# Sending every fourth row group of a column roll through SBUF

## The chip, the cores and the metric

The kernel runs on one core of a Trainium2 chip. A core has compute engines (TensorE, VectorE, ScalarE or ACT, GpSimd or POOL, SyncE or SP), an on-chip memory of 128 partitions (SBUF), and 16 DMA engines that move data between SBUF and the off-chip memory (HBM) or from HBM to HBM. SP, ACT and GpSimd each issue transfers on a queue ("ring") of their own, and each of the 16 DMA engines serves packets from all the rings. The metric is the device time in microseconds; the figure for a kernel is the median of several runs.

## The reference

```python
def setup_inputs():
    return {
        "x": np.random.randn(8192, 8192).astype(np.float32),
        "shift": 100,
    }

def reference(x, shift):
    return np.roll(x, shift, axis=1)
```

Every row of 8192 floats is rotated to the right by 100: the last 100 columns of `x` become the first 100 of the output. Nothing is calculated. 268.4 MB have to be read and 268.4 MB written.

## The kernel before

The columns of the output are cut at column `a` = 256. With a shift `s` of 100, `a` is the shift rounded up to a multiple of 128, plus 128; `g = a - s` = 156.

**The body, output columns 256 to 8191.** These come from `x` columns 156 to 8091, and are copied from HBM to HBM directly (line 43). The rows are cut into 128 blocks `c` of 64 rows, and each block into four groups `j`. A group has 16 rows (`e`), four rows apart, of 7936 floats: 16 pieces of 31,744 bytes, 496 KB in all, one piece for each DMA engine. There are 512 groups. Even `j` go to SP's ring and odd `j` to ACT's. In the last four blocks every group is cut into two halves by columns (at `mid`), which makes 16 groups into 32 transfers. So each ring gets 248 whole transfers and 16 halves. The compiled program makes each of these transfers wait until the transfer four places before it on its own ring has landed.

**The edge, output columns 0 to 255.** These hold the wrapped columns (0 to 99) and the first 156 columns of `x`. They go through SBUF on GpSimd's queue, in 16 tiles of 512 rows. For each tile there are three loads: most of it in one strip that runs across row ends, into `t` (line 72), the wrapped part of each fourth row into `h` (line 73), and the first 156 columns of each fourth row into `h` (line 76). VectorE then copies the parts of `t` into place in `h` (lines 74 and 77). The pools `reads` (for `t`) and `heads` (for `h`) have one buffer for each of the 16 tiles, so no load waits for a buffer. After all the loads are issued, 16 stores write the tiles to the output (line 80).

The two parts write different columns and nothing of one waits for the other. Only the DMA engines and HBM are shared.

Of the kernel before, what the change touches and what calls it, by code (L numbers as in the profile page):

```python
# [1 line left out]

# [4 lines left out]


@with_exitstack
def kernel(  # L10
    ctx: ExitStack,
    tc: tile.TileContext,
    x: bass.AP,
    shift: int,
    out: bass.AP,
):
    nc = tc.nc
    n_rows, n_cols = x.shape
    s = shift % n_cols
    a = -(-s // 128) * 128  # L20
    if 0 < a <= 384 and a + 128 <= n_cols:
        a += 128
    g = a - s
    P = nc.NUM_PARTITIONS
    engines = [nc.sync, nc.scalar]
    n_chunks = 16
    rows = n_rows // n_chunks

    xm = x.rearrange("(c e j) w -> c j e w", e=16, j=4)
    om = out.rearrange("(c e j) w -> c j e w", e=16, j=4)
    if a < n_cols:
        blocks = n_rows // 64
        mid = (a + n_cols) // 256 * 128
        for c in range(blocks):
            parts = ((a, mid), (mid, n_cols)) if c >= blocks - 4 and a < mid else ((a, n_cols),)  # L40
            for j in range(4):
                for lo, hi in parts:
                    engines[j % 2].dma_start(out=om[c, j, :, lo:hi], in_=xm[c, j, :, lo - s:hi - s])
    if a == 0:
        return


    if a > 512:
        for i in range(n_chunks):
            r = slice(i * rows, (i + 1) * rows)  # L50
            nc.gpsimd.dma_start(out=out[r, :s], in_=x[r, n_cols - s:])
            if g > 0:
                nc.gpsimd.dma_start(out=out[r, s:a], in_=x[r, :g])
        return

    Q = 4  # L60
    n_st = n_rows // (P * Q)
    reads = ctx.enter_context(tc.tile_pool(name="reads", bufs=n_st))
    heads = ctx.enter_context(tc.tile_pool(name="heads", bufs=n_st))
    xt = x.rearrange("(k p q) c -> k p q c", q=Q, p=P)
    ot = out.rearrange("(k p q) c -> k p q c", q=Q, p=P)
    tiles = []
    for k in range(n_st):
        t = reads.tile([P, Q - 1, a], x.dtype)
        h = heads.tile([P, Q, a], x.dtype)
        lead = bass.AP(tensor=x.tensor, offset=(k * P * Q + 1) * n_cols - s,  # L70
                       ap=[[Q * n_cols, P], [n_cols, Q - 1], [1, a]])
        nc.gpsimd.dma_start(out=t[:], in_=lead, single_packet=True)  # L72
        nc.gpsimd.dma_start(out=h[:, Q - 1, :s], in_=xt[k, :, Q - 1, n_cols - s:], single_packet=True)  # L73
        nc.vector.tensor_copy(h[:, :Q - 1, :s], t[:, :, :s])  # L74
        if g > 0:
            nc.gpsimd.dma_start(out=h[:, 0, s:], in_=xt[k, :, 0, :g], single_packet=True)  # L76
            nc.vector.tensor_copy(h[:, 1:, s:], t[:, :, s:])  # L77
        tiles.append(h)
    for k, h in enumerate(tiles):
        nc.gpsimd.dma_start(out=ot[k, :, :, :a], in_=h[:], single_packet=True)  # L80


# [1 line left out]
_INS = ['x', 'shift']  # L84
_OUTS = [((8192, 8192), 'float32')]

_NUMBERS = {'shift': 100}


# [26 lines left out]
```

## Time and profile before

| | |
|---|---|
| median of 3 runs | 818.49 us (817.95 to 818.54) |
| span of the profiled execution, first to last instruction | 813.9 us |
| GpSimd busy | 41.1 us, 68 instructions |
| VectorE busy | 12.0 us, 32 instructions |
| DMA packets | 22277, 276.90 MB, mean 340 GB/s |
| row copy, issue to landing | 12.5 us (median of 248 on each of SP and ACT), 496 KB each |
| half row copy, issue to landing | 5.9 us (16 on each ring) |
| edge store on GpSimd's queue, issue to landing | 102.9 us (median of 16), 512 KB each |
| first edge store issued | 255.5 us |
| last edge store issued | 403.4 us |
| sequencer time to issue one row copy | 510 ns on SP, 517 ns on ACT |

The span counts the instructions that the profiler recorded; what lies before the first and after the last of them is not in it. A DMA engine is counted as busy from the start of a packet to its end, whatever holds the packet up in between. The row "DMA" of the page gives this busy share for 40 equal slices of the span, and the row "GB/s" what was moved in each. A copy from HBM to HBM is counted once in GB/s, although it is both a read and a write of HBM; the page's last DMA row gives HBM's own reads and writes. The DMA view can be asked for any stretch of the span, and then gives each queue's packets, its MB and its share of the 16 engines' time in that stretch. Half of the packets of SP's and ACT's rings are of 4 bytes: each transfer ends on each engine with a write to a semaphore.

### The profile page before, as it was taken

The page shows a single profiled execution, that of the slowest core. Times are in us where ns is not written, and L with a number is a line of the kernel's source. Part 1 is how long each engine was busy: PE and PEld are TensorE (multiplying, and loading weights), DVE is VectorE, ACT ScalarE, POOL GpSimd, SP SyncE. Part 2 cuts the span into 40 slices and gives each one's busy share as a digit, 9 for nine tenths or more (in the row PEclk, how much of TensorE's full clock was granted, in tenths as well). Part 3 has the DMA queues.
Part 4 walks back from the last instruction along what each step waited for, and adds up shares of the span by engine and source line. Part 5 has one row for each costly group of instructions (what it writes and reads, how often), then busy time and mean ns, then how long its engine had stood idle before and what let it go on. Part 6 is the DMA issues. An engine that isn't in the chain of part 4 may idle for free. (4 is left out here: it accounts for less than half of the span.)

```text
span 813.9 us, 689 instructions
## 1 busy us (share of the span) xinstructions
DVE 12.0 (1%) x32; POOL 41.1 (5%) x68
## 2 busy tenths in 40 slices
DVE  0000000000000000000000000000000000000000
POOL 2000011111000100000000000000000000000000
DMA  9999999999999999999999999999999999999998
GB/s 314 346 340 344 353 346 350 344 351 344 346 355 346 345 362 354 353 357 354 355 355 349 342 335 331 335 332 325 335 328 332 334 337 334 332 337 332 334 314 293
DMA packets 22277, 276.90 MB, mean 340 GB/s; under 512 B 9472, under 2 KB 9728, under 8 KB 13824
## 3 DMA queue, kind: packets, MB, share of 16 engines
q1 hardware_dynamic: 8448, 130.04, 45.9%
q10 hardware_dynamic: 8448, 130.04, 44.3%
q0 software_dynamic: 5376, 16.78, 8.9%
q14 instruction: 5, 0.04, 0.0%
HBM read 268.44 MB, written 268.44 MB: 660 GB/s over the span
## 5 line engine op out<-in xcount | busy, mean ns | idle before, releaser
L80 POOL DMA_DIRECT2D out_dram<-h x16 | 11.4, 713 | 139.5 <-DMA out_dram<-h 92.5
L76 POOL DMA_DIRECT2D h<-in_x_dram x16 | 8.6, 540 | 158.4 <-DMA t<-in_x_dram 158.4
L72 POOL DMA_DIRECT2D t<-in_x_dram x16 | 12.2, 760 | 32.1 <-DMA h<-in_x_dram 31.3
L73 POOL DMA_DIRECT2D h<-in_x_dram x16 | 8.9, 558 | 32.7 <-DMA h<-in_x_dram 32.7
L74 DVE COPY h<-t 128x300 f32<-128x300 f32 x16 | 5.9, 367 | 268.4 <-DMA t<-in_x_dram 268.4
L77 DVE COPY h<-t 128x468 f32<-128x468 f32 x16 | 7.5, 468 | 0.0
L97 POOL MEMSET const-float32-0.0<- 128x1 f32 x1 | 0.1, 98 | 0.2 <-issue 0.2
L97 POOL MEMSET const-bfloat16-1.0<- 128x1 bf16 x1 | 0.1, 101 | 0.0
L97 POOL MEMSET const-float32-1.0<- 128x1 f32 x1 | 0.1, 98 | 0.0
L97 POOL MEMSET const-uint8-127<- 128x1 uint8 x1 | 0.1, 98 | 0.0
## 6 DMA issues: line engine op xcount, KB each, us to landing
out_dram<-in_x_dram ACTq DMA_DIRECT2D x248, 496.0 KB, 12.5
out_dram<-in_x_dram SPq DMA_DIRECT2D x248, 496.0 KB, 12.5
out_dram<-h POOLq DMA_DIRECT2D x16, 512.0 KB, 102.9
t<-in_x_dram POOLq DMA_DIRECT2D x16, 384.0 KB, 48.9
out_dram<-in_x_dram SPq DMA_DIRECT2D x16, 248.0 KB, 5.9
out_dram<-in_x_dram ACTq DMA_DIRECT2D x16, 248.0 KB, 5.9
h<-in_x_dram POOLq DMA_DIRECT2D x16, 78.0 KB, 41.9
h<-in_x_dram POOLq DMA_DIRECT2D x16, 50.0 KB, 47.2
```

The costliest lines, as they stand in the source:

```text
L72: nc.gpsimd.dma_start(out=t[:], in_=lead, single_packet=True)
L73: nc.gpsimd.dma_start(out=h[:, Q - 1, :s], in_=xt[k, :, Q - 1, n_cols - s:], single_packet=True)
L74: nc.vector.tensor_copy(h[:, :Q - 1, :s], t[:, :, :s])
L76: nc.gpsimd.dma_start(out=h[:, 0, s:], in_=xt[k, :, 0, :g], single_packet=True)
L77: nc.vector.tensor_copy(h[:, 1:, s:], t[:, :, s:])
L80: nc.gpsimd.dma_start(out=ot[k, :, :, :a], in_=h[:], single_packet=True)
L97: nc = _bacc.Bacc("TRN2", target_bir_lowering=False, num_devices=1)
```

## The change

The row groups are numbered in their old order and worked through in two rounds and a remainder. A round has 32 turns of three copies and one load, and then 32 turns of three copies and one store. The loads bring one group each (16 rows of 31,744 bytes) into SBUF; the stores write these groups to the output. So in each round 224 groups are done, 192 as copies and 32 through SBUF. Both rounds do 448 groups, 64 of them (1024 rows) through SBUF; the remaining 64 groups are copied as before, with the last 16 in halves.

Transfers alternate between SP and ACT, so that the fourth of each turn, the load or the store, is always ACT's. As compiled, SP has 280 whole copies and 16 halves; ACT has 152 whole copies, 16 halves, 64 loads and 64 stores, each load or store next to a copy.

A slab is an SBUF tile of 128 partitions by 7936 floats and holds eight groups. Group `n` takes the partitions `n % 8`, `n % 8 + 8`, and so on to 16 partitions. There are four slabs, 32 groups, and the second round uses them again.

To make room in SBUF the pools of the edge get 9 buffers instead of 16. So the edge's first stores are now issued among the loads: from the ninth tile on a store follows (line 121 of the changed kernel), and the last eight stores come at the end (line 123). In the compiled order of GpSimd's queue the first of these stores stands behind the loads of the ninth tile, and from the tenth tile on the load of `h` at line 114 waits for the store of the tile nine before it to land.

```diff
-        for c in range(blocks):
+        groups = [(c, j) for c in range(blocks) for j in range(4)]
+        held = 32 if 0 < a <= 512 and n_cols <= 8192 and blocks >= 16 else 0
+        pool = ctx.enter_context(tc.tile_pool(name="rows", bufs=4)) if held else None
+        width = n_cols - a
+        turn = 0
+
+        def issue(to, of):
+            nonlocal turn
+            engines[turn % 2].dma_start(out=to, in_=of)
+            turn += 1
+
+        def copy(c, j):
             parts = ((a, mid), (mid, n_cols)) if c >= blocks - 4 and a < mid else ((a, n_cols),)
-            for j in range(4):
-                for lo, hi in parts:
-                    engines[j % 2].dma_start(out=om[c, j, :, lo:hi], in_=xm[c, j, :, lo - s:hi - s])
+            for lo, hi in parts:
+                engines[turn % 2].dma_start(out=om[c, j, :, lo:hi], in_=xm[c, j, :, lo - s:hi - s])
+            issue_done()
...
+        def load(n, c, j):
+            if n % 8 == 0:
+                slabs.append(pool.tile([nc.NUM_PARTITIONS, width], x.dtype, name="slab"))
+            w = slabs[-1][n % 8::8, :]
+            issue(w, xm[c, j, :, a - s:n_cols - s])
+            return w
+
+        slabs = []
+        at = 0
+        for _ in range(2 if held else 0):
+            kept = []
+            for n in range(held):
+                for _ in range(3):
+                    copy(*groups[at])
+                    at += 1
+                kept.append((groups[at], load(n, *groups[at])))
+                at += 1
+            for (c, j), w in kept:
+                for _ in range(3):
+                    copy(*groups[at])
+                    at += 1
+                issue(om[c, j, :, a:], w)
+        for g_ in groups[at:]:
+            copy(*g_)
...
-    reads = ctx.enter_context(tc.tile_pool(name="reads", bufs=n_st))
-    heads = ctx.enter_context(tc.tile_pool(name="heads", bufs=n_st))
+    depth = min(n_st, 9)
+    reads = ctx.enter_context(tc.tile_pool(name="reads", bufs=depth))
+    heads = ctx.enter_context(tc.tile_pool(name="heads", bufs=depth))
...
-    for k, h in enumerate(tiles):
-        nc.gpsimd.dma_start(out=ot[k, :, :, :a], in_=h[:], single_packet=True)
+        if k >= depth - 1:
+            nc.gpsimd.dma_start(out=ot[k - depth + 1, :, :, :a], in_=tiles[k - depth + 1][:], single_packet=True)
+    for k in range(n_st - depth + 1, n_st):
+        nc.gpsimd.dma_start(out=ot[k, :, :, :a], in_=tiles[k][:], single_packet=True)
```

More of the change, by code (lines that the diff above doesn't have):

```diff
@@ L38, with issue_done @@
         mid = (a + n_cols) // 256 * 128
-        for c in range(blocks):
-            parts = ((a, mid), (mid, n_cols)) if c >= blocks - 4 and a < mid else ((a, n_cols),)
-            for j in range(4):
-                for lo, hi in parts:
-                    engines[j % 2].dma_start(out=om[c, j, :, lo:hi], in_=xm[c, j, :, lo - s:hi - s])
+        groups = [(c, j) for c in range(blocks) for j in range(4)]
[8 more added lines that the diff above has]
+        def copy(c, j):
+            parts = ((a, mid), (mid, n_cols)) if c >= blocks - 4 and a < mid else ((a, n_cols),)
+            for lo, hi in parts:
+                engines[turn % 2].dma_start(out=om[c, j, :, lo:hi], in_=xm[c, j, :, lo - s:hi - s])
+            issue_done()
+        def issue_done():
+            nonlocal turn
+            turn += 1
+        def load(n, c, j):
[21 more added lines that the diff above has]
+            copy(*g_)
     if a == 0:
```

## The prediction

> **What bounds the kernel now.** I read the page's engine part first. VectorE is busy 12.0 us and GpSimd 41.1 us of a span of 813.9 us, so no compute engine matters. The chain of waits is of little use here: it follows GpSimd's queue and stops at 403.41 us, half the span before the end. So I went to the DMA rows:
>
> ```profile
> DMA  9999999999999999999999999999999999999998
> GB/s 314 346 340 344 353 346 350 344 351 344 346 355 346 345 362 354 353 357 354 355 355 349 342 335 331 335 332 325 335 328 332 334 337 334 332 337 332 334 314 293
> q1 hardware_dynamic: 8448, 130.04, 45.9%
> q10 hardware_dynamic: 8448, 130.04, 44.3%
> q0 software_dynamic: 5376, 16.78, 8.9%
> HBM read 268.44 MB, written 268.44 MB: 660 GB/s over the span
> ```
>
> The 16 DMA engines always have a packet in hand: 45.9 + 44.3 + 8.9 = 99.1% of their time. q1 and q10 are the rings of SP and ACT (which is which does not matter here), q0 is GpSimd's. The bytes per second are not constant: about 350 GB/s while q0 runs, about 332 after. "Busy" engines may still be held up by something outside them, so I compared stretches with and without q0's traffic. The DMA view for 50 to 250 us, for 300 to 400 us, and for 550 to 800 us:
>
> ```profile
> q1 hardware_dynamic: 1979, 31.40, 41.5%
> q10 hardware_dynamic: 1978, 31.37, 39.3%
> q0 software_dynamic: 2470, 6.75, 19.0%
> ```
>
> ```profile
> q1 hardware_dynamic: 978, 15.52, 46.0%
> q10 hardware_dynamic: 980, 15.59, 42.2%
> q0 software_dynamic: 1181, 4.30, 12.4%
> ```
>
> ```profile
> q1 hardware_dynamic: 2761, 41.38, 49.5%
> q10 hardware_dynamic: 2755, 41.59, 49.2%
> ```
>
> A byte of q1 or q10 is read from HBM and written to HBM; a byte of q0 touches HBM once, with SBUF on its other side. HBM traffic is thus 2 x (q1 + q10) + q0: (2 x 62.77 + 6.75) MB / 200 us = 661 GB/s, (2 x 31.11 + 4.30) / 100 = 665, and 2 x 82.97 / 250 = 664. Three stretches, three mixes, one HBM rate, while the bytes through the engines go 348, 354, 332 GB/s. The packet records say the same: the shortest packet of 31,744 bytes takes 1.173 us, the mean is 1.507 us from 550 to 780 us (20% under 1.18 us) and 1.348 us from 50 to 400 us (39%). The engines are stretched by what lies behind them. HBM traffic sets the time, and the engines have room: 16 x 31,744 B / 1.173 us = 433 GB/s at their shortest packet.
>
> **The change, part by part.** 64 of the 512 row groups (64 x 507,904 B = 32.5 MB) stop being one copy each and become a load into SBUF and, 64 ACT transfers later, a store. HBM traffic stays at 536.9 MB. The engines carry 32.5 MB more: 576 full packets for each engine where there were 512.
>
> *The legs.* Price of a copied MB, from the last stretch: 250 / 82.97 = 3.013 us. Price of an SBUF MB, as what the other stretches leave: (200 - 62.77 x 3.013) / 6.75 = 1.61 us and (100 - 31.11 x 3.013) / 4.30 = 1.46 us; both together 1.55. Half of a copy would be 1.51. A staged MB costs two legs: 2 x 1.55 - 3.01 = 0.09 us more, times 32.5 = **+3 us**. The ends by the two rows are +7 and -3 us.
>
> *The engines' room.* If HBM stays at 664 GB/s, three copies and one leg (seven HBM units, four engine units) need 664 x 4/7 = 379 GB/s of engine work, and 394 where q0 adds its 34 GB/s; the trace shows at most 354 without loss. In time: each engine has 512 packets in the two rounds and 64 in the remainder. With q0's 72 us (8.9% of 813.9) as they are and the remainder at 1.507 us, the 512 must average about (810 - 72 - 96) / 512 = 1.25 us, close to the shortest, 1.173. From below the loss is 0, as the step from 332 to 354 GB/s lost nothing. From above: if packets get no quicker than the 1.348 us already seen, 512 x 1.348 + 96 + 72 = 858 us, against 99.1% of 813.9 = 807 now, +52. I take **+7 us**, nearer to the rows that lost nothing but not on them, since the room left is about a third of what it was in the mixed stretch (0.08 against 0.175 us over the shortest). This choice is a judgement.
>
> *Issues.* SP issues 296 transfers instead of 264, ACT the same 296. At 0.51 us each that is 151 us of 814, hidden under the 12.5 us to landing of the four transfers in flight on each ring; uncovered, the 32 more would cost 16 us on each. In the compiled order every ring transfer waits for the one four places before it on its ring, before and after. The added waits are weak: a store stands 64 ACT transfers behind its load, some 170 us at 810 us / 296 = 2.7 us each; the second round's first load stands 50 behind the last store out of its slab, some 130 us. Were one late, ACT's later copies would queue behind it while SP went on. Cost 0.
>
> *GpSimd's queue.* With 9 buffers, the edge stores of L80 start among the loads, and from the tenth tile on each load of h waits until the store of the tile nine before has landed; behind it in that queue stand the next loads and stores, and VectorE's copies wait for those loads. As compiled these waits come in four pairs. At most each costs one landing (102.9 us): nine tiles take about 9/16 of 255 us = 143 us, plus 4 x 103, plus the last eight stores at 102.9 us = 658 us. The cover is the row copies, which run to the end; past 814 us every microsecond would count. Cost 0.
>
> Sum: 813.9 + 3 + 7 = 824 us of span. The runs' median is 818.49, 4.6 us over this span, for start and last landing outside it. Forecast: **828 us**.
>
> **Rivals.**
> (a) *SBUF side too narrow.* A load goes to 16 partitions, eight apart, one row from each engine. If two engines share a way into SBUF, a leg takes up to 2 x 1.173 = 2.35 us. 128 legs at 2.35 = 301, 448 copies at 1.18 = 529, q0 between 40 (its 4,096-byte packets at their median 0.16 us, scaled to 16.78 MB) and 72: 870 to 902 us, plus 4.6. Half of the legs meeting gives 128 x 1.76 + 529 + 56 = 810 with every copy at its shortest, and with these at 1.25 us 841, so 845. For: no transfer of this trace goes to so few partitions. Against: the other ring lets engines drift apart. The point from which it decides: legs above about 1.5 us. I work with 850 to 885.
> [...]
> (b) *Faster: a leg costs less than half a copy.* The legs are packets of 31,744 B, q0's are of 4 KB or less, and a staged row is read and written at different times. For: the 300 to 400 us row (1.46). Against: the other. As far below half as the 1.61 row lies above gives -7 us and no loss of room: **811**; twice that is 804.
> (c) *The engines are the bound after all*, a leg costing a packet like a copy: 576 x 1.434 (90.2% of 813.9 / 512) + 72 = 898, so 903. For: 99.1% busy. Against: the three HBM sums.
> That the change is not what it says is excluded by the compiled order: 64 loads and 64 stores alternate with copies on ACT.
>
> **How the numbers follow.** Forecast 0.52 (its own range 816 to 842), (a) 0.14, (b) 0.29, (c) 0.05. A measurement of this kernel tells about 0.2%, 1.6 us, from no change. Forecast: 0.41 slower, 0.08 within, 0.03 faster; (b): 0.02 within, 0.27 faster; (a) and (c) slower. Together slower 0.60, same 0.10, faster 0.30. Range 805 to 868: down to nearly twice (b), up into (a); (c), the rest of (a) and a bit of (b) stay out.
>
> **What would show it.** Right: HBM traffic near 655 GB/s and engine bytes of 370 to 390 GB/s in the rounds (to about 690 us), 332 after; packet mean near 1.27 us in the rounds; q0 done before 660 us. (a): packets of ACT's ring much longer than SP's, with a group near 2.3 us. (b): HBM traffic above 670 GB/s in the rounds. (c): engine bytes stay at 350 or below. Wrong altogether: gaps in the DMA row, or a queue other than the two rings landing last.

## The result, and the profile after

The changed kernel takes 825.75 us (median of 5 runs, 823.73 to 830.82) where the kernel before took 818.49 us on the same chip (817.95 to 818.62). The ratio is 1.0104, with a 95% interval of 1.0073 to 1.0136: about 7 us slower by the medians. The profiled execution is the slowest of the five, 830.82 us with a span of 829.0 us. The runs spread over 7.1 us, where those of the kernel before spread over 0.67 us here and over 2.1 to 5.5 us on the chips of the experiments. In the experiments, a ratio leaves out runs that took over 1.5% longer than the fastest of their kernel, and a time in us is the median of all runs.

The DMA rows of the page:

```profile
DMA  9999999999999999999999999999999999999998
GB/s 316 353 363 354 352 361 391 386 401 383 384 392 402 382 389 392 391 396 381 404 398 392 396 379 377 377 378 382 385 380 377 381 378 378 378 354 325 326 314 300
q10 hardware_dynamic: 9472, 146.30, 47.1%
q1 hardware_dynamic: 9472, 146.30, 46.5%
q0 software_dynamic: 5376, 16.78, 6.1%
HBM read 268.44 MB, written 268.44 MB: 648 GB/s over the span
```

The engines are as busy as before and HBM moves the same bytes; q1 and q10 carry 32.5 MB more. The GB/s row has three levels: 352 to 363 in the slices from 21 to 124 us, 381 to 404 up to 476 us, 377 to 385 up to 725 us, the end of the rounds. A slice is 20.7 us. The view of the tile `slab` shows which stage is where (columns: issue time in ns, then start of the first and the last):

```profile
L47 ACTq DMA_DIRECT2D slab<-in_x_dram x64: 515/522/866, 1.4 to 551.3; - x64
L47 ACTq DMA_DIRECT2D out_dram<-slab x64: 527/527/537, 193.5 to 722.7; - x64
DMA to landing us min/median/max: 8.7/11.2/14.0
```

The first round's loads run from 1.4 to about 190 us. So the low level covers the first half of these loads, and ends with no stage of the kernel.

To see what HBM did, the bytes need a weight. A copy touches HBM twice, a load or a store once: 2 x 227.54 MB of copies, 65.01 MB of loads and stores and 16.78 MB of the edge make 536.87 MB, and the page has 2 x 268.44 = 536.88. In the rounds one of four ring transfers is a load or a store, so four parts through the rings are seven parts of HBM. HBM traffic in the rounds is therefore 7/4 x (q1 + q10) + q0, and before it was 2 x (q1 + q10) + q0. The DMA view from 20 to 115 us, of the changed kernel and then of the kernel before:

```profile
q10 hardware_dynamic: 967, 15.21, 46.4%
q1 hardware_dynamic: 974, 15.43, 41.6%
q0 software_dynamic: 1112, 3.03, 12.2%
```

```profile
q1 hardware_dynamic: 939, 14.92, 40.8%
q10 hardware_dynamic: 936, 14.83, 39.5%
q0 software_dynamic: 1143, 3.11, 19.5%
```

(7/4 x 30.64 + 3.03) / 95 us = **596 GB/s** after, (2 x 29.75 + 3.11) / 95 = **659 GB/s** before. In these 95 us the changed kernel moved 56.65 MB of HBM traffic where the other moved 62.61: it fell behind by 5.96 MB, which at 659 GB/s is 9.0 us. The changed kernel from 350 to 500 us, and then from 520 to 740 us:

```profile
q10 hardware_dynamic: 1676, 26.70, 45.9%
q1 hardware_dynamic: 1678, 26.67, 45.5%
q0 software_dynamic: 1513, 5.29, 9.4%
```

```profile
q1 hardware_dynamic: 2628, 41.75, 50.7%
q10 hardware_dynamic: 2624, 41.56, 49.3%
```

That is (7/4 x 53.37 + 5.29) / 150 = 658 and 7/4 x 83.31 / 220 = 663 GB/s, against 661 to 665 in the stretches of the kernel before that the prediction used. So of the 15.1 us by which the two profiled spans differ, 9.0 arose from 20 to 115 us. The first 20 us add 1.7 us (10.9 MB of HBM traffic against 12.1 MB), and some 5 us came at a slightly lower rate from 115 to 500 us (252.6 MB against 255.8 MB). Once GpSimd's queue is empty, at 499 us, the rounds run at HBM's old rate. The medians differ by only half of 15.1 us: this profile is of the slowest of the five runs, and that of the kernel before is of a run faster than all five timed ones (813.9 us of span and some 1.8 us around it). So the figures of this section show where the loss lies, and overstate how large it usually is.

Why the first loads? The packet records give durations. At the start the 16 engines are in step (the 16 packets of the first load start within 0.7 us of one another), so that the whole packets of ACT's ring, sorted by start and cut into sixteens, are its transfers one by one; every second is a load. By the fifth load the starts lie 2.5 us apart, so the later columns are less sure. The first five loads took, in us as a mean of 16 packets:

```
                                    load 1  load 2  load 3  load 4  load 5
changed kernel, step of 8 partitions  1.96    1.92    1.91    2.04    1.74
step of 8, 28 groups held             1.87    1.85    1.78    1.68    1.60
step of 7, 28 groups held             1.74    1.75    1.72    1.35    1.39
step of 1                             3.66    3.54    3.28    3.41    2.85
changed kernel without the edge       1.99    1.82    1.61    1.43    1.34
kernel before, copies in these places 1.52    1.24    1.28    1.35    1.28
```

The copies between these loads on the same ring (q10) took 1.18 us in the changed kernel, and 1.23 us the first of them, close to the shortest packet, 1.173 us. In step, a load is the slow transfer. The last row shows that the first place is slow even for a plain copy. The rows between are of the experiments.

The long packets last as long as the low level of the GB/s row. From 20 to 115 us, 18% of ACT's whole packets took over 1.9 us and their mean was 1.46 us, against 1.29 us on SP's ring; from 130 to 190 us, with the same round of loads still running, 2% did.

### The profile page after: what moved, and what is told of

The parts are those of the page before. It is cut to its first block, busy times and chain, and to the rows that moved or that the text cites. A ratio compares the mean times of both kernels' runs of the same rounds, so it can differ in the third digit from the quotient of the medians.

```text
span 829.0 us, 762 instructions
## 1 busy us (share of the span) xinstructions
DVE 12.0 (1%) x32; POOL 41.5 (5%) x68
## 3 DMA queue, kind: packets, MB, share of 16 engines
q0 software_dynamic: 5376, 16.78, 6.1%
HBM read 268.44 MB, written 268.44 MB: 648 GB/s over the span
## 6 DMA issues: line engine op xcount, KB each, us to landing
out_dram<-slab ACTq DMA_DIRECT2D x64, 496.0 KB, 10.9
```

## The experiments

Three groups of runs were made on chips where the kernel before took 817.06, 828.81 and 828.51 us, and one run on a chip where it took 829.31, so ratios are compared, not times.

### The partitions that a load goes to

Two kernels differ only in the step between partitions. A slab takes seven groups so that both fit.

```diff
-        held = 32 if 0 < a <= 512 and n_cols <= 8192 and blocks >= 16 else 0
+        held = 28 if 0 < a <= 512 and n_cols <= 8192 and blocks >= 16 else 0
-            if n % 8 == 0:
+            if n % 7 == 0:
-            w = slabs[-1][n % 8::8, :]
+            w = slabs[-1][n % 7:n % 7 + 106:7, :]     # step of 7
+            w = slabs[-1][n % 7::8, :]                # or: step of 8, the control
```

> The changed kernel with 28 groups held in a round instead of 32, seven to a slab, and a load's 16 rows seven partitions apart instead of eight. In the changed kernel's profile the first loads, with the 16 engines in step, take 1.91 to 2.04 us a packet where the copies beside them take 1.18 to 1.4. Theory A (the 16 partitions share too few ways into SBUF): a step of seven shares fewer, so the first loads fall towards 1.2 to 1.4 us, HBM traffic from 20 to 115 us rises from 596 to about 650 GB/s and the loss of 7 us shrinks to 0 to 3: 818 to 822 us. Theory B (the engines have too little room left, wherever the rows go): no difference from the same kernel with a step of eight, about 825 us, HBM traffic from 20 to 115 us near 600 GB/s. [...]

> The control for the step of seven: 28 groups held in a round, seven to a slab, rows eight partitions apart. Both theories: like the changed kernel, 824 to 826 us, first loads near 1.9 to 2.0 us, HBM traffic near 600 GB/s from 20 to 115 us.

Step of seven: 819.83 us, ratio 1.0034 (1.0021 to 1.0047). Step of eight: 822.31 us, ratio 1.0074 (1.0052 to 1.0096); that is below the 824 to 826 us expected of the control. The DMA view from 20 to 115 us, step of seven and then step of eight:

```profile
q1 hardware_dynamic: 1066, 16.92, 44.0%
q10 hardware_dynamic: 1057, 16.64, 43.1%
q0 software_dynamic: 1176, 3.19, 12.9%
```

```profile
q10 hardware_dynamic: 1028, 16.32, 46.4%
q1 hardware_dynamic: 1027, 16.29, 43.4%
q0 software_dynamic: 1116, 2.99, 10.7%
```

HBM traffic is (7/4 x 33.56 + 3.19) / 95 = 652 GB/s with a step of seven and 632 with eight, where 600 was expected of the control. Each is of the slowest run of its kernel, and two kernels with a step of eight gave 596 and 632, so the times weigh more than these rates. The intervals of the ratios do not overlap, and nothing but the partitions differs: about half of the control's loss hangs on where the rows land in SBUF. The first loads did not fall as far as theory A expected: three at 1.72 to 1.75 us, not 1.2 to 1.4, and only from the fourth on near 1.4. So a load in step stays long with a step of seven as well; a part of that may be what made a plain copy take 1.52 us in the first of these places.

The third kernel puts a group into 16 neighbouring partitions:

```diff
-            w = slabs[-1][n % 8::8, :]
+            w = slabs[-1][n % 8 * 16:n % 8 * 16 + 16, :]
```

> The changed kernel with the 16 rows of a group in 16 neighbouring partitions. Theory A: more rows share a way into SBUF, a leg takes up to 4 x 1.17 = 4.7 us where engines meet, 128 legs of 4.7 and 448 copies of 1.2 to 1.4 us are 1140 to 1230 us an engine at the worst, and above 880 us anyhow. Theory B: no change, about 825 us. [...]

865.52 us (857.44 to 876.68), ratio 1.0512 (1.0487 to 1.0537). Theory A has the direction, gave up to 4.7 us for the loads, of which the first four took 3.3 to 3.7 us, and overrated the sum. The GB/s row of its page, of the slowest run, shows why:

```profile
GB/s 236 276 259 271 285 280 307 313 343 374 386 383 394 385 378 393 392 378 393 364 394 405 392 383 367 367 367 374 386 381 382 379 382 380 388 360 325 329 319 297
```

A slice is 21.9 us. The loss lies in the first nine slices, the first round of loads. The second round's loads, into neighbouring partitions as before, run at 364 to 405 GB/s. The packets agree: of ACT's whole packets 44% took over 1.9 us from 20 to 170 us, and 8% from 440 to 590 us, in the second round's loads. So the long packets grow rare while the partitions stay the same. That loads are long while the engines arrive together, and that these later arrive in turns, is a reading of these figures; the turns were not measured.

### A head start of plain copies

```diff
         at = 0
+        for g_ in groups[:48] if held else []:
+            copy(*g_)
+            at += 1
```

> The changed kernel with 48 plain groups moved from the end to the front, so that the first load is issued some 75 us later, when the 16 engines have had time to drift apart. Theory C (the loss needs the 16 engines in step, as they are at the start): the stretch at 596 GB/s goes or gets much shorter, 818 to 821 us. Theory D (whatever the engines' order, a first round of loads costs 95 us at 596 GB/s): the slow stretch moves to about 75 to 190 us, and the time stays near 825 us.

821.91 us, ratio 1.0061 (1.0045 to 1.0078), against 1.0104 (1.0073 to 1.0136) of the changed kernel; the two intervals just touch. The DMA view from 85 to 180 us, where the first loads now are:

```profile
q10 hardware_dynamic: 1074, 17.08, 47.4%
q1 hardware_dynamic: 1075, 17.08, 43.5%
q0 software_dynamic: 998, 3.01, 9.7%
```

HBM traffic is (7/4 x 34.16 + 3.01) / 95 = 661 GB/s: the slow stretch is gone in this profile, which is of the fastest run where that of the changed kernel is of the slowest. The time is a little above theory C's 818 to 821; some loss remains elsewhere.

> Rows in 16 neighbouring partitions, with 48 plain groups first (865 us without these). In the profile without them the slow stretch lasts about 200 us and the second round of loads costs nothing. Theory C (what matters is that the engines start in step; the drift that plain copies bring is enough): 822 to 830 us. Theory D (the engines are sorted into turns by meeting at SBUF, and plain copies don't do that): the slow stretch follows later and is nearly as long, 845 to 865 us.

The time is 855.50 us on a chip where the kernel before took 828.81 us. With neighbouring partitions the ratio falls from 1.0512 to 1.0291 (1.0251 to 1.033), between the two theories, whose times are for the chip of 817.06 us: a head start takes away some two fifths of the loss and does not remove it.

> Both cures together: rows seven partitions apart (28 held, seven to a slab) and 48 plain groups moved to the front. Theory A (the loss is the sharing of ways into SBUF while engines meet, and nothing else; a leg is otherwise worth half a copy): ratio to the kernel before 0.998 to 1.002, HBM traffic 660 to 665 GB/s from 75 us on. Theory B (beside that, the smaller room of the engines costs something that no layout cures): 1.003 to 1.006, HBM traffic in the rounds 650 to 657.

Ratio 1.0034 (1.0018 to 1.0051), the same as the step of seven alone. This favours theory B, though its interval just reaches theory A's 1.002: something is left that neither this step nor the start removes.

### The edge's new order alone

The kernel before with nine buffers and the earlier stores:

```diff
-    reads = ctx.enter_context(tc.tile_pool(name="reads", bufs=n_st))
-    heads = ctx.enter_context(tc.tile_pool(name="heads", bufs=n_st))
+    depth = min(n_st, 9)
+    reads = ctx.enter_context(tc.tile_pool(name="reads", bufs=depth))
+    heads = ctx.enter_context(tc.tile_pool(name="heads", bufs=depth))
...
```

> The kernel before with the edge's nine buffers and earlier stores alone; no row goes through SBUF. Both theories: no change, ratio 0.998 to 1.002, since GpSimd's transfers end long before the row copies. If the edge's new order had a part in the loss, 1.003 or more.

Ratio 1.0008 (0.9994 to 1.0022): this part of the change costs nothing that can be measured. The interval of the kernel with both cures, 1.0018 to 1.0051, just overlaps it. This kernel is also the base for the one with both cures, on the same chip and with the same edge. From 130 to 450 us, this kernel and then the one with both cures:

```profile
q1 hardware_dynamic: 3104, 49.34, 44.6%
q10 hardware_dynamic: 3104, 49.21, 43.1%
q0 software_dynamic: 3635, 11.89, 12.6%
```

```profile
q1 hardware_dynamic: 3523, 55.94, 45.3%
q10 hardware_dynamic: 3524, 55.91, 44.0%
q0 software_dynamic: 3550, 11.55, 11.1%
```

HBM traffic is 653 and 648 GB/s: in these two profiles 0.8% less over 320 us, 2.5 us, nearly all of what is left (0.34% of 829 us is 2.8). After the edge has ended the two are equal. This kernel from 520 to 720 us and the one with both cures from 500 to 700 us:

```profile
q1 hardware_dynamic: 2062, 32.70, 50.5%
q10 hardware_dynamic: 2064, 32.83, 48.5%
```

```profile
q10 hardware_dynamic: 2357, 37.37, 50.3%
q1 hardware_dynamic: 2360, 37.46, 50.2%
```

That is 2 x 65.53 / 200 = 655 GB/s without rounds and 7/4 x 74.83 / 200 = 655 with.

### How much room the engines have

The kernel with both cures, and a load or store as every second transfer instead of every fourth, in four rounds:

```diff
-        for _ in range(2 if held else 0):
+        for _ in range(4 if held else 0):
...
-                for _ in range(3):
+                for _ in range(1):
```

> Rows seven partitions apart, 48 plain groups first, and every second transfer of a round a load or a store instead of every fourth: four rounds of 28, 112 groups through SBUF, all on ACT's ring, where SP has copies alone. HBM at 664 GB/s would need 664 x 2/3 = 443 GB/s of engine work, more than the 433 of the shortest packets. Theory A (engine room costs nothing until it is used up): the rounds run at 425 to 433 GB/s of engine work, 227.5 MB in 525 to 535 us against 514 at HBM's rate, so 11 to 21 us slower, 828 to 840 us. Theory B (a cost that grows as the room shrinks): engine work stays at 400 or below, 55 us or more slower, above 870 us.

902.73 us, ratio 1.088 (1.0851 to 1.0908). The time is theory B's. The DMA view from 500 to 700 us, with the edge ended:

```profile
q1 hardware_dynamic: 2552, 40.51, 50.9%
q10 hardware_dynamic: 2550, 40.45, 49.2%
```

The engines move 80.96 MB / 200 us = 405 GB/s, 94% of what their shortest packets would give and a little above theory B's 400, and HBM traffic is 3/2 of that, 607 GB/s. So HBM, at 655 GB/s in other kernels on this chip, is no longer what limits. The 405 is a mean of two stages: 395 GB/s from 550 to 600 us, in a round of loads, and 415 from 650 to 700 us, in the stores. With the edge running, from 225 to 425 us, the same kernel moves 373 GB/s. There is thus no single ceiling of the engines; whether the SBUF side or the engines themselves set these figures was not separated.

### The edge left out

Three kernels without the edge's code: the kernel before, the one with the step of seven, and the changed kernel. None writes output columns 0 to 255.

```diff
-    Q = 4
-    n_st = n_rows // (P * Q)
-    depth = min(n_st, 9)
...
```

> The kernel before without the edge: output columns 0 to 255 are not written, and GpSimd and VectorE have no work. It is the base for the two runs beside it. HBM traffic falls from 536.9 to 520.1 MB, so by HBM's rate the ratio to the kernel before is 520.1 / 536.9 = 0.969 to 0.975.

> The kernel with rows seven partitions apart (ratio 1.0034 with the edge) without the edge: columns 0 to 255 are not written. Theory B (what is left of the loss comes where GpSimd's traffic takes the engines' last room, 390 GB/s and more of 433): without that traffic the engine work stays near 380 and the time equals the kernel before without the edge within 0.2%. Theory E (a staged row costs a little more than a copied one by itself): 0.3% above it, as with the edge.

> The changed kernel (rows eight partitions apart) without the edge: columns 0 to 255 are not written. If the slow first 100 us come of the row loads alone, they stay: 0.6 to 1.0% above the kernel before without the edge. If they need GpSimd's loads into SBUF at the same time, the loss goes: within 0.2% of it.

800.73 us, 799.20 us and 800.05 us; as ratios to the whole kernel before 0.9667 (0.9654 to 0.9680), 0.9645 (0.9632 to 0.9658) and 0.9660 (0.9641 to 0.9678). Without GpSimd's traffic the kernels with rows through SBUF are not slower: the step of seven is 0.2% faster by medians, with intervals that just overlap, and the step of eight is level, not the 0.6 to 1.0% slower that loads alone would give. From 20 to 115 us, the changed kernel without the edge and then the kernel before without it:

```profile
q10 hardware_dynamic: 1123, 17.81, 51.3%
q1 hardware_dynamic: 1124, 17.84, 49.1%
```

```profile
q10 hardware_dynamic: 978, 15.37, 52.1%
q1 hardware_dynamic: 988, 15.68, 48.4%
```

7/4 x 35.65 / 95 = 657 GB/s against 2 x 31.05 / 95 = 654. The first load is as long as ever (1.99 us, in the table above), but nothing is lost. The slow first 95 us need both, the long loads and the edge's traffic. Two readings remain: at 375 GB/s of engine work there is slack to make up for long loads, and without the edge the loads grow short sooner (1.43 us by the fourth, 2.04 with the edge). These runs do not separate them.

### One round after the edge has ended

```diff
-        held = 32 if 0 < a <= 512 and n_cols <= 8192 and blocks >= 16 else 0
+        held = 24 if 0 < a <= 512 and n_cols <= 8192 and blocks >= 16 else 0
-        for _ in range(2 if held else 0):
+        for g_ in groups[:328] if held else []:
+            copy(*g_)
+            at += 1
+        for _ in range(1 if held else 0):
```

> The changed kernel's layout (rows eight partitions apart) with the edge, but with one round of 24 groups only, placed after 328 plain groups, so that it begins some 520 us in, when GpSimd's traffic has ended. Theory B (the loss comes only where GpSimd's traffic and the row legs together use up the engines' room): ratio to the kernel before 0.998 to 1.002, HBM traffic in the round as in the plain stretches. Theory E (each group through SBUF costs its share, 1.04% x 24 / 64 = 0.39%): 1.003 to 1.005.

Ratio 0.9994 (0.9982 to 1.0006). The DMA view from 550 to 750 us, inside the round:

```profile
q10 hardware_dynamic: 2359, 37.49, 51.1%
q1 hardware_dynamic: 2356, 37.40, 49.3%
```

7/4 x 74.89 / 200 = 655 GB/s, the rate of the kernel with the edge's new order alone, on a chip of nearly the same speed (828.81 and 829.31 us for the kernel before). The engines do 375 GB/s of work there. With the edge whole and the partitions as in the changed kernel, a late round costs nothing that can be measured, and gains nothing either. The first load of this kernel comes at 540 us, when the edge is done and the engines have long been under way; this run does not tell which of the two matters.

No version tried that writes the whole output beats the kernel before by more than the measurement tells.

## Why the prediction came out as it did

**HBM traffic as the bound: held.** Wherever the engines have room, HBM traffic stands at its old rate whatever the mix: 663 GB/s from 520 to 740 us at 379 GB/s of engine work, just the 379 that the prediction worked out.

**The price of a leg, +3 us (-3 to +7): within its range, and the +3 itself was not seen.** With nothing beside them, 64 groups through SBUF changed the time by 800.05 - 800.73 = -0.7 us, 56 in the better layout by -1.5 us, neither clear of the noise.

**The engines' room, +7 us: the size came out near by luck, and the shape was not right.** The prediction spread a small loss over all the rounds, and chose its size by judgement between 0 and 52. Its reason for the choice has a slip: 0.08 us of room against 0.175 is nearly a half, not a third. The medians differ by 7 us, so with the legs at nothing this term alone has the size of the whole loss. On the profiled execution it is 10.7 us in the first 115 us, some 5 us in the rest of the time that the edge runs, and nothing later. The 433 GB/s that the prediction set as the limit was not reached: with every second transfer a load or a store it was 395 to 415. 379 GB/s costs nothing. 386 GB/s with the edge (the kernel with both cures, 130 to 450 us) goes with 0.8% of the rate lost. The prediction did weigh the edge's 34 GB/s in its 394, and that part matters: without the edge the loss is gone. What it did not have is that the loss needs long loads too, which it had put to rival (a).

**Rival (a), SBUF too narrow: the partitions have a part in the loss, but not at the rival's price.** Loads in step took 1.91 to 2.04 us, over the 1.5 us that the prediction gave as the point from which it decides, and a step of seven takes away about half of the loss. It gave 850 to 885 us for engines that meet all through the rounds; in fact the long loads last for some 100 us. Without the edge even those cost nothing. So the forecast's number held while a part of the loss came where the rival looked for it. The kernel with neighbouring partitions shows a large price for the choice of partitions: 865.52 us, ratio 1.0512.

That engines share a way into SBUF, and how many do at each step, was the author's assumption. No run shows it, nor the two terms taken from it, 2 x 1.173 = 2.35 us in the prediction and 4 x 1.17 = 4.7 us in an expectation. What the runs showed in their place: the first four loads took 1.91 to 2.04 us in the changed kernel and 3.3 to 3.7 us in neighbouring partitions, 1.6 to 1.7 and 2.8 to 3.1 times the shortest packet. With a step of seven the first three took 1.72 to 1.75 us and the next two 1.35 and 1.39. The ratios have the same order: 1.0034 with a step of seven, 1.0074 and 1.0104 with eight, 1.0512 with one.

**Rival (b), faster: not in this kernel.** The step of seven without the edge was 0.2% faster, which is within the noise. HBM traffic in the rounds stood at 656 to 663 GB/s after the slow stretch, where (b) said above 670.

**Rival (c), a leg costs like a copy: no.** Engine bytes rose to 377 to 404 GB/s after the slow stretch, where it said 350 or below.

**The rest.** GpSimd's queue at no cost held (1.0008), and so did the weak waits on the slabs: loads and stores on ACT's ring land in 11.2 us and the engines stay busy. GpSimd's queue was done at 499 us, before the 660 that the prediction allowed. Some small things were off. The 4.6 us between span and median is not all overhead: the profiled execution after took 830.82 us with a span of 829.0, so some 1.8 us lie around a span, and the profiled execution of before must have been a fast one. The whole packets of the rounds took 1.32 us as a mean, not 1.27, and GpSimd's packets took 6.1% of the engines' time, 51 us, where the prediction kept 72. And the rounds end at about 725 us, not 690: 448 groups alone take 685 us at 664 GB/s of HBM traffic, the edge's 16.8 MB another 25, and the loss the rest.

What stays open: why the long loads end after some 100 us in the changed kernel and some 200 with neighbouring partitions, what lengthens loads in step and how the partitions come into it, whether the edge takes away the engines' slack or keeps the loads long, and why the runs of the changed kernel spread over 7.1 us. An order among the engines that settles differently from run to run would fit the first and the last, but was not measured.

## What to carry to other kernels

Weigh DMA bytes by how often they touch HBM, stretch by stretch: if that sum is constant while the engines' GB/s changes, a detour through SBUF that saves no HBM bytes cannot pay by itself, and it can cost by the room of the engines that it takes (ratio 1.088 with every second transfer a load or a store). Here the detour was free beside the copies (800.05 us against 800.73, both without the edge) and cost beside the copies and GpSimd's queue (ratio 1.0104); place it where the other queue is idle, and choose the partitions that its rows go to (ratio 1.0034 seven apart, 1.0512 side by side). And a loss of 1% may be a loss of 10% in a tenth of the time: look at the rate by stretch before spreading an estimate over the whole.

## What the hardware showed that was not expected

- Sixteen rows sent to 16 neighbouring partitions, by engines in step, took 3.3 to 3.7 us a packet of 31,744 bytes in the first four loads, where 1.173 us is the shortest; in the second round of such loads the engines moved 364 to 405 GB/s.
- Where every second transfer was a load or a store and GpSimd's queue was empty, the engines moved 395 GB/s in a stage of loads and 415 in a stage of stores, where the shortest packets say 433.
- In the kernel with neighbouring partitions and in the changed kernel, the stores out of SBUF never showed a slow stretch (364 to 405 and 377 to 404 GB/s from the first store to the last), and the first loads did. But neither issued a store near the start, where the engines are in step: the first stores come at 235 and 194 us.
